# A hybrid mixer layer on one core: the input loaded with channels on the partitions, and three orders stated

## The chip, the core and the metric

The kernel runs on one core of one Trainium2 chip. The metric is device time of one execution in microseconds (us); lower is better. An execution is profiled apart, and its trace is what the views below show. The engines are named as in the profile: PE is TensorE (PEld its weight loads), DVE is VectorE, ACT is ScalarE, POOL is GpSimd, SP is SyncE, which issues most DMAs.

## What is computed

One inference step of one layer with shared weights, over 128 context tokens and 512 latent tokens, 640 together, of width 1024:

```python
def _trunk_layer(x, mod, g_pre, w_in, ...):
    shift, scale, gate = jnp.split(mod, 3, axis=-1)
    h = _rmsnorm(x, g_pre) * (1 + scale) + shift
    proj = h @ w_in
    qa, ka, va, ga, qr, zf, zb, ir, gr, uf, gf = _split_columns(proj)
    ...
    oa = _neighbourhood_attention(...)       # context attention for the context tokens
    o_r, s_fin = _hgrn_bidir(qr, zf, zb, ir, lb_f, lb_b, s0)
    o_r = _rmsnorm(o_r, g_hgrn.reshape(R_HEADS, R_VAL_DIM)).reshape(B, N, R_WIDTH).astype(x.dtype)
    o_f = _fourier(uf, w_fnet)
    mixed = jnp.concatenate([oa * silu(ga), o_r * silu(gr), o_f * silu(gf)], axis=-1)
    out = mixed @ w_out
    return x + gate * _rmsnorm(out, g_post), ka, va, s_fin
```

`mod` is `silu(c) @ w_ada + b_ada`, one vector of 3072 for the context and one for the latent tokens. The first norm is over the 1024 channels of a token: `x * rsqrt(mean(x*x) + 1e-6) * g`.

## The kernel before, in words

All large matrix products are made in single-pass matmuls on operands split into a high and a low part (`hi` and `lo` of a weight, `hT[0]` and `hT[1]` of the modulated input), three matmuls for one product (`mm3`, line 210). An input block of 128 columns is 8 channel tiles x 2 token halves x 3 = 48 matmuls of 128x320.

**The start** (`start_stream`, line 244). The input `x` is loaded with tokens on the partitions, five tiles of 128 tokens, each in two pieces `xa` (640 channels) and `xb` (384 channels) (`load_x`, 217). `scale_x` (222) sums the squares of a tile, `xa` on ScalarE and `xb` on VectorE, takes root and reciprocal, and multiplies the tile by it. Then, for each of the eight channel tiles k, here called a round:

- two blocks of `w_ada` (`wss`, 512 KB each, line 178 loads them) are multiplied with the SiLU of the two conditioning vectors (`mod_cols`, 195, through line 113): 16 matmuls of 32 weight columns, 32 instructions in the trace. This is called the mod group of k;
- VectorE copies the sums (`row`, 266), TensorE transposes the two halves (line 127), VectorE reduces them (272) and makes the scale `G` and the shift (273 to 275);
- `modulated` (233) transposes the five 128x128 pieces of x on TensorE, ScalarE applies scale and shift out of PSUM (237 for the latent tokens, 239 for the context), VectorE makes the high part (240) and the low part (241) of `hT`.

`zf_stream` (286) multiplies each finished channel tile with the first two input blocks, zf0 and zf1, whose weights VectorE and ScalarE split (lines 130, 131): 12 matmuls of 128x320 a round. `fill` (965) then runs the other blocks one after the other, beginning with zb0; `recurrence` (423) and `attention` (645) are streams of their own, put between the blocks' matmuls by modelled times (`Order`, 39), and the framework's scheduler then sets the order on each engine. Engines work their own lists in order.

**The recurrence's states.** After seven levels of 64x128 matmuls, which VectorE merges (458), the chunk states are made: `pst` holds products in one of five PSUM buffers of the tag "b", VectorE copies the final state out (519) and updates the other states one after the other (532), reading `pst`. While it does so the other recurrence's level work (474 to 483) stands in VectorE's list too.

`by_token` (346) copies the last transposed piece of a value tile into a small tile of the pool "m" when `copy_last` is set. Constants (`const`, 137) are loaded by GpSimd's queue, `cc` and `lbl` by SyncE's. The lower bounds `lb` are made first of all (154 to 160).

Of the kernel before, what the change touches and what calls it, by code (L numbers as in the profile page):

```python
# [9 lines left out]
F32 = mybir.dt.float32  # L10
# [3 lines left out]
ALU = mybir.AluOpType  # L14
# [57 lines left out]
def mixer_kernel(ctx: ExitStack, tc: tile.TileContext, A, O):  # L72
# [51 lines left out]

    def tr(out, src):
        od.now += 0.107
        last_tr[0] = te.transpose(out, src, ident).ins  # L127

    def split(src, hi, lo, hi_eng=None, lo_eng=None):
        (sc.copy if hi_eng is None else hi_eng.tensor_copy)(hi, src)  # L130
        (ve if lo_eng is None else lo_eng).tensor_sub(lo, src, hi.bitcast(F32))  # L131
# [15 lines left out]
    sel = const("sel", [2, P])  # L147
# [3 lines left out]


    lb, lb1 = const("lb", [2, 2]), const("lb1", [2, 2])
    ve.tensor_sub(lb, lbl, lbl)
    sc.activation(lb, lb, ACT.Exp)
    ve.reciprocal(lb1, lb)
    ve.tensor_mul(lb, lb, lb1)
    ve.tensor_sub(lb, lb, lb)
    ve.tensor_scalar_max(lb, lb, 0.0)
    ve.tensor_scalar(lb1, lb, -1.0, 1.0, op0=ALU.mult, op1=ALU.add)  # L160
# [10 lines left out]
    sc.activation(csil[:, :, 0:2], cc, ACT.Silu)  # L171

    wdma, nb = [], [1]
# [7 lines left out]
    def split_w(raw, lo_eng=None, shape=(KT, P), tags=("hi", "lo")):  # L181
        hi, lo = [wp.tile([P, *shape], F32R, tag=t, name=nm(t), bufs=WB[t]) for t in tags]
        split(raw, hi, lo, lo_eng=lo_eng)
        return hi, lo
# [10 lines left out]
    def mod_cols(out, w, chain):  # L195

        t = od.now
        for k in range(KT):
            run_mm(chain, out[32 * (k % 4):32 * (k % 4) + 32, :], csil[:, k, :], w[:, k, :], start=(k < 4), stop=(k >= 4))
        od.now = t + 0.45  # L200
# [3 lines left out]
    xa, xb = [T(tag="xa") for _ in range(5)], [T(384, tag="xb") for _ in range(5)]  # L204

    def xcols(i, k):
        return (xa[i] if k < 5 else xb[i])[:, k % 5 * P:k % 5 * P + P]
# [9 lines left out]
    def load_x():  # L217
        for i in range(5):
            load(xa[i], A["x"][i * P:(i + 1) * P, 0:NT])
            load(xb[i], A["x"][i * P:(i + 1) * P, NT:D])  # L220

    def scale_x():
        for i in range(5):
            ss2 = S(2)
            sc.activation(T(), xa[i], ACT.Square, accum_out=ss2[:, 0:1])
            ve.tensor_tensor_reduce(PE_()[:, 0:384], xb[i], xb[i], 1.0, 0.0, op0=ALU.mult, op1=ALU.add,
                                    accum_out=ss2[:, 1:2])
            ve.tensor_add(rstd[:, i:i + 1], ss2[:, 0:1], ss2[:, 1:2])
            rsqrt_mean(rstd[:, i:i + 1], D)
            ve.tensor_scalar(xa[i], xa[i], rstd[:, i:i + 1], 0.0, op0=ALU.mult, op1=ALU.add)  # L230
            ve.tensor_scalar(xb[i], xb[i], rstd[:, i:i + 1], 0.0, op0=ALU.mult, op1=ALU.add)

    def modulated(k, pm):
        h, px = T(), PB()
        for i in range(1, 5):
            tr(px[:, (i - 1) * P:i * P], xcols(i, k))
        sc.activation(h[:, P:NT], px, ACT.Identity, bias=shift[:, k, 1:2], scale=G[:, k, 1:2])
        tr(pm[:, 384:512], xcols(0, k))
        sc.activation(h[:, 0:P], pm[:, 384:512], ACT.Identity, bias=shift[:, k, 0:1], scale=G[:, k, 0:1])
        ve.tensor_copy(hT[0][:, k, :], h)  # L240
        ve.tensor_sub(hT[1][:, k, :], h, hT[0][:, k, :].bitcast(F32))
        od.set(f"h{k}", LAT["h"])

    def start_stream():
        load_x()
# [10 lines left out]
        scale_x()  # L256
        od.now = 11.0
        for k in range(KT):
# [4 lines left out]
            for u in range(2):  # L263
                mod_cols(pm[:, u * P:(u + 1) * P], raws[2 * k + u], [])
            yield 0
            ve.tensor_copy(row, pm[:, 0:256])
            yield LAT["row"]

            for u in range(2):
                tr(pm[:, u * P:(u + 1) * P], row[:, u * P:(u + 1) * P])  # L270
            pt = S(4)
            ve.reduce_sum(pt, pm[:, 0:256].rearrange("p (u g r) -> p u r g", u=2, r=32)[:, :, 0:2, :], axis=AX.X)
            ve.tensor_scalar(G[:, k, :], pt[:, 0:2], bss[:, k, 0:1], 1.0, op0=ALU.add, op1=ALU.add)
            ve.tensor_scalar_mul(G[:, k, :], G[:, k, :], gpre[:, k:k + 1])  # L274
            ve.tensor_scalar_add(shift[:, k, :], pt[:, 2:4], bss[:, k, 1:2])
            modulated(k, pm)
            if k < 2:
                zf_w.append(split_w(zraw[k]))
# [67 lines left out]
    def by_token(src, copy_last=False):  # L346
# [5 lines left out]
        if copy_last:  # L352
            last = S(P)
# [69 lines left out]
    def recurrence(p):  # L423
# [88 lines left out]
        for d in range(2):  # L512
# [5 lines left out]
            for hh in range(2):  # L518
                ve.tensor_copy(fin[RS[hh], :], pst[RS[hh], 64 * hh:64 * hh + 64])
# [3 lines left out]
            for a, i in enumerate(order[d]):  # L523
                for hh in range(2):
# [4 lines left out]
                    else:  # L529
                        ip = order[d][a - 1]  # L530
                        cs = slice((a - 1) * P + 64 * hh, (a - 1) * P + 64 * hh + 64)
                        ve.scalar_tensor_tensor(sall[r, cdst], sall[r, cs], Td[r, ip:ip + 1], pst[r, cdst],  # L532
                                                op0=ALU.mult, op1=ALU.add)
# [319 lines left out]
    def gate_vectors():  # L853
        selr = cp.tile([P, 2, P], F32R, tag="selr", name="selr")
# [219 lines left out]
def prepare(inp):  # L1074
    inp = {k: np.asarray(v) for k, v in inp.items()}
    r = _consts()
    r["x"] = np.concatenate([inp["x_prompt"][0], inp["x_sample"][0]], 0)
    r["cc"] = np.stack([inp["c_ctx"], inp["c"][0]], -1).reshape(KT, P, 2).transpose(1, 0, 2)
# [59 lines left out]
```

## Time and profile before

| | |
|---|---|
| median of 3 runs | 434.32 us (433.76 to 434.38) |
| profiled execution, its own time | 434.13 us |
| its span in the trace | 432.3 us |
| PE busy | 409.4 us (95%) |
| DVE busy | 303.0 us (70%) |
| ACT busy | 205.8 us (48%) |
| HBM read, written | 43.80 MB, 3.28 MB |
| time outside the span (434.13 - 432.3) | 1.8 us |

The trace counts from the span's start. A view of the timeline gives a start, a duration, the engine, the line in the code, what is written and read, and in brackets the idle time ahead of it with what ended it. The chain of waits follows the work that ended last back to the start, so that its pieces leave no gap; for matmuls its pieces are the better measure of a group, since one matmul's own duration overlaps the next one's.

### The profile page before, as it was taken

What the parts mean: (1) busy time and instruction counts of PE and PEld (TensorE: products, weight loads), DVE (VectorE), ACT (ScalarE), POOL (GpSimd) and SP (SyncE); (2) the same over time, 40 slices, a digit from 0 to 9 for tenths busy, and PEclk for the clock granted to TensorE, in tenths of its full rate; (3) what the DMA queues carried; (4) which work ended last, traced back from release to release, by engine and by line L of the source; (5) the groups of instructions that cost most, each with busy time, mean ns of one, the idle gap of its engine ahead of it and who ended that gap; (6) DMA issues with size and microseconds to landing.
All of it is one profiled execution on the core that took longest, in us unless ns stands there. A gap on an engine that the chain in (4) does not pass through costs nothing.

```text
span 432.3 us, 8308 instructions
## 1 busy us (share of the span) xinstructions
PE 409.4 (95%) x3176; PEld 372.6 (86%) x3176; DVE 303.0 (70%) x866; ACT 205.8 (48%) x551; POOL 7.4 (2%) x23
## 2 busy tenths in 40 slices
PE   0699999999998999999999999999999999999994
PEld 0488999999988998999899989899898889988884
DVE  3775579999896966885598657786679748471164
ACT  6525466566342526754445634744466553341331
POOL 2000000000020000000000000000000000000000
PEclk9999999999999999999999999999999999999998
DMA  7996154101202021122012522245323202245032
GB/s 236 414 407 237 49 176 141 61 16 50 99 12 75 9 62 49 56 98 74 33 60 72 143 73 90 90 154 159 105 101 122 89 9 102 85 156 198 0 147 99
DMA packets 19528, 47.62 MB, mean 110 GB/s; under 512 B 3184, under 2 KB 6912, under 8 KB 19488
## 3 DMA queue, kind: packets, MB, share of 16 engines
q1 hardware_dynamic: 19376, 46.94, 31.3%
q8 instruction: 25, 0.41, 0.4%
q0 software_dynamic: 112, 0.14, 0.3%
q14 instruction: 15, 0.12, 0.1%
HBM read 43.80 MB, written 3.28 MB: 109 GB/s over the span
## 4 chain that ended last, share of the span: by engine, by line
PE 90%; DVE 4%; DMA 3%; ACT 1%; issue 0%; SPq 0%; DVEq 0%
PE pb L113 84%; PE pb L127 7%; DMA vs<-wss 1%; DMA txa<-x 1%; DVE t L532 1%; DVE AL L458 1%; DVE AL L495 0%; ACT L688 0%; DVE lo L131 0%; DVE t L960 0%; ACT hi L130 0%; ACT pe L688 0%; ACT pe L689 0%; DVE t L475 0%; DVE t L474 0%
## 5 line engine op out<-in xcount | busy, mean ns | idle before, releaser
L113 PE MATMUL pb<-hT,hi 128*128 128x320 f32 x896 | 207.8, 316 | 0.5 <-DVE t L131 0.4
L113 PEld LDWEIGHTS pb<-hT,hi 128*128 128x128 f32 x896 | 149.5, 188 | 6.4 <-issue 1.1
L113 PE MATMUL pb<-hT,lo 128*128 128x320 f32 x448 | 139.7, 313 | 0.0
L113 PEld LDWEIGHTS pb<-hT,lo 128*128 128x128 f32 x448 | 84.1, 188 | 1.4 <-DVE G L274 0.2
L131 DVE TENSOR_TENSOR lo<-raw,hi 128x1024 fp32r<-128x1024 f32 x35 | 42.7, 1221 | 21.8 <-ACT hi L130 21.5
L130 ACT CAST hi<-raw 128x1024 fp32r<-128x1024 f32 x35 | 36.7, 1049 | 35.2 <-PE pb L113 19.5
L113 PE MATMUL pb<-t,t 64*128 64x128 f32 (+2 forms) x414 | 43.1, 291 | 1.9 <-DVE t L532 1.5
L113 PEld LDWEIGHTS pb<-t,t 64*128 64x128 f32 (+1 forms) x414 | 36.2, 188 | 6.3 <-issue 2.3
L113 PE MATMUL pb<-hi,mh 128*128 128x512 f32 (+1 forms) x108 | 32.1, 376 | 0.0
L130 ACT CAST pT<-pb 128x256 fp32r<-128x256 f32 x64 | 22.9, 371 | 16.3 <-DVE pT L131 9.8
L131 DVE TENSOR_TENSOR pT<-pb,pT 128x256 fp32r<-128x256 f32 x64 | 26.3, 416 | 1.6 <-ACT pT L130 1.3
L113 PEld LDWEIGHTS pb<-hi,mh 128*128 128x128 f32 x108 | 19.4, 189 | 3.2
L113 PE MATMUL pb<-pT,mh 128*128 128x512 f32 (+1 forms) x102 | 22.2, 364 | 0.0
L688 ACT ACTIVATE pe<-pb,s 128x256 f32<-128x256 f32 x32 | 15.2, 476 | 13.0 <-DVE s L687 7.7
L127 PE MATMUL pb<-ident,pe 128*128 128x128 f32 x136 | 20.8, 274 | 0.5 <-ACT pe L689 0.5
L943 ACT ACTIVATE t<-pb 128x512 f32<-128x512 f32 (+1 forms) x11 | 6.0, 551 | 30.5 <-PE pb L113 30.5
L113 PEld LDWEIGHTS pb<-pT,mh 128*128 128x128 f32 x102 | 17.7, 189 | 3.1
L113 PE MATMUL pb<-lo,mh 128*128 128x512 f32 (+1 forms) x54 | 20.2, 373 | 0.0
L127 PEld LDWEIGHTS pb<-ident,pe 128*128 128x128 f32 x136 | 16.5, 140 | 1.7 <-ACT pe L689 0.7
L458 DVE COPY_PREDICATED AL<-masks,pb 128x512 f32<-128x512 uint32 x24 | 16.5, 738 | 1.9 <-PE pb L113 1.8
L113 PE MATMUL pb<-pT,vs 128*128 128x256 f32 (+1 forms) x96 | 17.2, 321 | 0.0
L699 DVE TENSOR_TENSOR o<-pb,o 64x512 f32<-64x512 f32 (+1 forms) x16 | 7.8, 487 | 13.3 <-ACT o L698 13.2
(209 smaller groups left out, 630.1 us busy)
## 6 DMA issues: line engine op xcount, KB each, us to landing
raw<-win SPq DMA_DIRECT2D x30, 512.0 KB, 3.3
pT<-wss SPq DMA_DIRECT2D x12, 512.0 KB, 10.2
raw<-wg SPq DMA_DIRECT2D x8, 512.0 KB, 3.4
raw<-wout SPq DMA_DIRECT2D x8, 512.0 KB, 3.3
t<-x SPq DMA_DIRECT2D x10, 256.0 KB, 5.8
o_y<-t SPq DMA_DIRECT2D x9, 256.0 KB, 2.1
vs<-wss SPq DMA_DIRECT2D x4, 512.0 KB, 9.1
tbl<-tbl SPq DMA_DIRECT2D x4, 512.0 KB, 3.3
```

The lines of the kernel that those rows point to most:

```text
L113: return te.matmul(out, lhsT, rhs, start=start, stop=stop).ins
L127: last_tr[0] = te.transpose(out, src, ident).ins
L130: (sc.copy if hi_eng is None else hi_eng.tensor_copy)(hi, src)
L131: (ve if lo_eng is None else lo_eng).tensor_sub(lo, src, hi.bitcast(F32))
L458: ve.copy_predicated(out, mk.to_broadcast([P, i1 - i0, P]), src)
L532: ve.scalar_tensor_tensor(sall[r, cdst], sall[r, cs], Td[r, ip:ip + 1], pst[r, cdst], op0=ALU.mult, op1=ALU.add)
L688: sc.activation(pe[:, 256:512], ss[:, 256:512], ACT.Exp, bias=m[:, 1:2], accum_out=m[:, 3:4])
L699: ve.tensor_add(out, src[r, :], out)
L943: sc.activation(T(512)[:, cs], po[:, 0:cs.stop - cs.start], ACT.Square, accum_out=ssb[:, j:j + 1])
```

## The change

The input is also prepared as `xT`, eight tiles with 128 channels on the partitions and the 640 tokens along the free axis, and loaded as such, first on SyncE's queue. The 40 transposes of x are gone. The squares of all eight tiles are made on ScalarE, added on VectorE, and summed over the partitions by five small matmuls with a column of ones; root and reciprocal are taken once for all five token tiles; five transposes of a broadcast bring the inverse norms to every partition, and ScalarE copies them to `rb`. VectorE multiplies each `xT` tile by `rb`, one round ahead. ScalarE applies scale and shift from SBUF and, from k = 2 on, also makes the high part of `hT`. `G` is made in one instruction where there were two. The order of these steps on ScalarE, VectorE and TensorE is stated by dependencies without a semaphore (`turn`). `lbl` and `cc` are loaded by ScalarE's queue, `sel` later by SyncE's; the lower bounds are made behind the squares. The states' copies and updates get a high priority on VectorE, and `by_token` copies its last piece in place.

```diff
-    cc = const("cc", [KT, 2], dma=sy.dma_start)
-    lbl = const("lbl", [2, 2], dma=sy.dma_start)
+    xT, x_last = [], None
+    for k in range(KT):
+        xT.append(T(tag="xT"))
+        with tc.issue_after(x_last) if x_last else ExitStack():
+            x_last = sy.dma_start(xT[k], A["xT"][k]).ins
+    lbl = const("lbl", [2, 2], dma=sc.dma_start)
+    cc = const("cc", [KT, 2], dma=sc.dma_start)
...
+    def inverse_norms():
+        acc = T()
+        last = sc.activation(S(1), eps, ACT.Silu)
+        last = turn(sc.activation(acc, xT[0], ACT.Square), last)
+        for k in range(1, KT):
+            sq = T()
+            last = turn(sc.activation(sq, xT[k], ACT.Square), last)
+            added = ve.tensor_add(acc, acc, sq)
+            if k == 4:
+                last = turn(sc.activation(csil[:, :, 0:2], cc, ACT.Silu), last)
+        lower_bounds(last, added)
+        pn = PB()
         for i in range(5):
+            mm(pn[:, 2 * i:2 * i + 2], acc[:, i * P:(i + 1) * P], ones)
+        sc.activation(rstd, pn[...], ACT.Sqrt, bias=eps, scale=1.0 / D)
+        ve.reciprocal(rstd, rstd)
+        return pn
+
+    def spread_norms(pn, prev):
+        pr = PB()
         for i in range(5):
+            tr((pr if i < 4 else pn)[:, i % 4 * P:i % 4 * P + P], rstd[:, i:i + 1].to_broadcast([P, P]))
+            if i == 0:
+                turn_names(last_tr[0], prev)
+        rb = T()
+        sc.copy(rb[:, 0:512], pr)
+        return rb, sc.copy(rb[:, 512:NT], pn[:, 0:P])
...
-        for i in range(1, 5):
-            tr(px[:, (i - 1) * P:i * P], xcols(i, k))
-        sc.activation(h[:, P:NT], px, ACT.Identity, bias=shift[:, k, 1:2], scale=G[:, k, 1:2])
-        tr(pm[:, 384:512], xcols(0, k))
-        sc.activation(h[:, 0:P], pm[:, 384:512], ACT.Identity, bias=shift[:, k, 0:1], scale=G[:, k, 0:1])
-        ve.tensor_copy(hT[0][:, k, :], h)
-        ve.tensor_sub(hT[1][:, k, :], h, hT[0][:, k, :].bitcast(F32))
+        sc.activation(h[:, P:NT], xT[k][:, P:NT], ACT.Identity, bias=shift[:, k, 1:2], scale=G[:, k, 1:2])
+        h_act[0] = sc.activation(h[:, 0:P], xT[k][:, 0:P], ACT.Identity, ...)
+        if k < 2:
+            h_hi[0] = ve.tensor_copy(hT[0][:, k, :], h)
+        else:
+            sc.copy(hT[0][:, k, :], h)
+        return ve.tensor_sub(hT[1][:, k, :], h, hT[0][:, k, :].bitcast(F32))
...
+            row_done = ve.tensor_scalar(G[:, k, :], pt[:, 0:2], bsc1[:, k:k + 1], gpre[:, k:k + 1], op0=ALU.add, op1=ALU.mult)
+            h_done = modulated(k)
+            if k + 1 < KT:
+                turn(ve.tensor_mul(xT[k + 1], xT[k + 1], rb), row_done)
...
-            last = S(P)
+            last = src[:, 4 * P:5 * P]
...
+            with tc.high_priority():
+                for hh in range(2):
+                    ve.tensor_copy(fin[RS[hh], :], pst[RS[hh], 64 * hh:64 * hh + 64])
...
+                        with tc.high_priority():
+                            ve.scalar_tensor_tensor(sall[r, cdst], sall[r, cs], Td[r, ip:ip + 1], pst[r, cdst],
+                                                    op0=ALU.mult, op1=ALU.add)
```

How the change stands in the engines' lists is shown at three places. The numbers behind names are those of buffers and differ between the kernels.

TensorE's list in round 3, before: `vs` and `pT` are the blocks of `w_ada`, `csil` the conditioning vectors, `txa` the tiles of x, `hT` the modulated input, `hi` the weights of zf0 and zf1.

```order
L113 MATMUL pb_347<-pT_197,csil 32x128 x8
L113 MATMUL pb_347<-pT_199,csil 32x128 x8
L127 MATMUL pb_379<-ident,txa_108 128x128
L127 MATMUL pb_379<-ident,txa_109 128x128
L127 MATMUL pb_379<-ident,txa_110 128x128
L127 MATMUL pb_379<-ident,txa_111 128x128
L127 MATMUL pb_300<-ident,txa_107 128x128
L113 MATMUL pb_117<-hT_105,hi_240 128x320
...
L127 MATMUL pb_347<-ident,row_346 128x128 x2
```

The same place in the changed kernel:

```order
L113 MATMUL pb_322<-pT_178,csil 32x128 x8
L113 MATMUL pb_322<-pT_180,csil 32x128 x8
L113 MATMUL pb_115<-hT_113,hi_227 128x320
L113 MATMUL pb_116<-hT_113,hi_227 128x320
...
L136 MATMUL pb_322<-ident,row_321 128x128 x2
L113 MATMUL pb_369<-vs_231,csil 32x128 x8
```

The five transposes of x between the mod group and the zf matmuls are gone, the two of `row` stay.

ScalarE's list around h5, before: `raw_645` is the weight block zb0, `G` and `shift` belong to the round, L283 is a Sigmoid whose table is loaded ahead of use.

```order
L237 ACTIVATE t_425<-pb_426,shift,G 128x512
L239 ACTIVATE t_425<-pb_394,shift,G 128x128
L237 ACTIVATE t_474<-pb_475,shift,G 128x512
L283 ACT_TABLE_LOAD
L283 ACTIVATE s_485<-G 128x1
L239 ACTIVATE t_474<-pb_443,shift,G 128x128
L130 CAST hi_647<-raw_645 128x1024
L237 ACTIVATE t_519<-pb_520,shift,G 128x512
```

In the changed kernel (`txT_86` is the tile of k = 4, `txT_88` of k = 5, `raw_541` is zb0):

```order
L272 ACTIVATE t_399<-txT_86,shift,G 128x512
L273 ACTIVATE t_399<-txT_86,shift,G 128x128
L277 CAST hT_113<-t_399 128x640
L139 CAST hi_543<-raw_541 128x1024
L272 ACTIVATE t_442<-txT_88,shift,G 128x512
L273 ACTIVATE t_442<-txT_88,shift,G 128x128
L330 ACT_TABLE_LOAD
L330 ACTIVATE s_448<-G 128x1
L277 CAST hT_113<-t_442 128x640
L272 ACTIVATE t_487<-txT_90,shift,G 128x512
```

The split of zb0 now stands ahead of h5, where it stood ahead of h6, and each round has a cast more.

TensorE's list near the states of the first recurrence, before: `t,t` matmuls are the last level of the other recurrence, `hT` matmuls belong to input blocks.

```order
L113 MATMUL pb_1566<-t_1481,t_1482 128x128
L113 MATMUL pb_1772<-hT_106,hi_1664 128x320
...
L113 MATMUL pb_1772<-hT_105,lo_1665 128x320
L113 MATMUL pb_1565<-t_1481,t_1482 128x128
L113 MATMUL pb_1838<-hT_105,hi_1834 128x320
```

In the changed kernel:

```order
L113 MATMUL pb_1510<-t_1425,t_1426 128x128
L113 MATMUL pb_1715<-hT_114,hi_1608 128x320
...
L113 MATMUL pb_1715<-hT_113,lo_1609 128x320
L113 MATMUL pb_1781<-hT_113,hi_1777 128x320
...
L113 MATMUL pb_1781<-hT_113,lo_1778 128x320
L113 MATMUL pb_1509<-t_1425,t_1426 128x128
L113 MATMUL pb_1781<-hT_113,hi_1777 128x320
```

The last level matmul (`pb_1565`, now `pb_1509`) had eight `hT` matmuls ahead of it since the one before, and now has 26. On VectorE the copies and updates of the states keep their places between the other recurrence's level steps; two low parts of `vs` and one merge of 128x512 (line 505) now stand among them, ahead of the last update.

More of the change, by code (lines that the diff above doesn't have):

```diff
@@ L127, in tr, with split @@
         last_tr[0] = te.transpose(out, src, ident).ins
[L129 to L131 removed]
+    def split(src, hi, lo, hi_eng=None, lo_eng=None, prev=None, lo_prev=None):
+        ins = (sc.copy if hi_eng is None else hi_eng.tensor_copy)(hi, src)
+        if prev is not None:
+            turn(ins, prev)
+        ins = (ve if lo_eng is None else lo_eng).tensor_sub(lo, src, hi.bitcast(F32))
+        if lo_prev is not None:
+            turn(ins, lo_prev)
     ident = cp.tile([P, P], F32, tag="ident", name="ident")
@@ L141, in const @@
         return t
-    cc = const("cc", [KT, 2], dma=sy.dma_start)
-    lbl = const("lbl", [2, 2], dma=sy.dma_start)
+    xT, x_last = [], None
[5 more added lines that the diff above has]
+    cc = const("cc", [KT, 2], dma=sc.dma_start)
     bss = const("bss", [KT, 2])
     gpre = const("gpre", [KT])
-    sel = const("sel", [2, P])
+    bsc1 = const("bsc1", [KT])
+    ve.tensor_scalar(bsc1, bss[:, :, 0], 1.0, 0.0, op0=ALU.add, op1=ALU.add)
+    ones = cp.tile([P, 2], F32, tag="ones", name="ones")
+    ve.memset(ones, 1.0)
     RS = [slice(0, 64), slice(64, 128)]
@@ L170, in mixer_kernel @@
     gp.memset(csil, 0.0)
-    sc.activation(csil[:, :, 0:2], cc, ACT.Silu)
-    wdma, nb = [], [1]
+    wdma, nb = [x_last], [1]
     def load_raw(src, tag, shape=(KT, P)):
@@ L193, in load, with mod_cols @@
             sy.dma_start(t, src)
-    def mod_cols(out, w, chain):
+    def mod_cols(out, w, chain, prev=None):
         t = od.now
@@ L199, in mod_cols @@
             run_mm(chain, out[32 * (k % 4):32 * (k % 4) + 32, :], csil[:, k, :], w[:, k, :], start=(k < 4), stop=(k >= 4))
+            if k == 0 and prev is not None:
+                turn_names(chain[0], prev)
         od.now = t + 0.45
@@ new lines, in lower_bounds @@
+    def lower_bounds(prev, added):
+        ve.tensor_sub(lb, lbl, lbl)
+        turn(sc.activation(lb, lb, ACT.Exp), prev)
+        turn(ve.reciprocal(lb1, lb), added)
+        ve.tensor_mul(lb, lb, lb1)
+        ve.tensor_sub(lb, lb, lb)
+        ve.tensor_scalar_max(lb, lb, 0.0)
+        ve.tensor_scalar(lb1, lb, -1.0, 1.0, op0=ALU.mult, op1=ALU.add)
+    def inverse_norms():
[10 more added lines that the diff above has]
+        pn = PB()
+        for i in range(5):
+            mm(pn[:, 2 * i:2 * i + 2], acc[:, i * P:(i + 1) * P], ones)
+        sc.activation(rstd, pn[:, 0:10].rearrange("p (i two) -> p i two", two=2)[:, :, 0], ACT.Sqrt, bias=eps, scale=1.0 / D)
+        ve.reciprocal(rstd, rstd)
+        return pn
@@ L853, in gate_vectors @@
     def gate_vectors():
+        sel = const("sel", [2, P], dma=load)
         selr = cp.tile([P, 2, P], F32R, tag="selr", name="selr")
```

67 lines of the change are left out of this document (28 added, 39 removed).

## The prediction

> **What bounds the kernel now.** I read the page first, for which engine fills the span: busy us, share of the span, instructions.
>
> ```profile
> PE 409.4 (95%) x3176; PEld 372.6 (86%) x3176; DVE 303.0 (70%) x866; ACT 205.8 (48%) x551; POOL 7.4 (2%) x23
> ```
>
> Of the span of 432.3 us TensorE idles for 22.9. The view of waits, for TensorE alone, says where.
>
> ```profile
> PE pb L113 <- DMA vs<-wss: 14.0, 1, 14.0
> PE pb L113 <- DVE t L532: 1.5, 1, 1.5
> PE pb L127 <- ACT pe L689: 0.5, 1, 0.5
> ```
>
> 14.0 us lie ahead of its first matmul, which waits for the first block of w_ada, and 1.5 us in the recurrence, where a matmul waits for the state updates of line 532; the attention part loses 0.5. From the first matmul on TensorE is hardly ever without work. So a matmul taken out is worth its own time, if nothing else comes late in its place. Whether it does is a question for the start, so I looked at two stretches of it.
>
> ```profile
> 30.00:35.00 5.00, 5.00 (x81) 4.46 (x83) 2.81 (x10) 1.23 (x2) 0.00 (x0) 1.00 1.03 410
> 40.00:45.00 5.00, 4.99 (x59) 4.27 (x59) 2.85 (x8) 4.57 (x7) 0.00 (x0) 1.00 0.01 3
> ```
>
> The columns are stretch, length, busy time of PE, PEld, DVE, ACT, POOL, granted clock, DMA share, GB/s. In the first the DMAs run full at 410 GB/s, so that a round's 1.05 MB of w_ada takes 2.6 us; in the second they have nothing left to do. TensorE is full in both, and slower than the DMAs: the chain of waits shows a round.
>
> ```profile
> 18.12 1.01 PE pb L113 x16
> 19.14 1.27 PE pb L127 x5
> ...
> 27.03 1.01 PE pb L113 x32
> 28.04 0.70 PE pb L127 x5
> 28.74 1.76 PE pb L113 x12
> ...
> 38.88 0.81 PE pb L127 x6
> ...
> 43.48 0.70 PE pb L113 x4
> ```
>
> Mod group 1.01, twelve zf matmuls 1.76, two row transposes 0.27 (0.81 / 6 is 0.135 each) and five of x 0.68: 3.72 us. The zf matmuls of k = 5 begin at 43.48, 16.45 us after the mod group of k = 3 at 27.03. The first rows go at half pace: sixteen instructions of a mod group took 1.01 us at 18.12, where thirty-two took as much at 27.03, and five transposes 1.27 us at 19.14 and 0.70 at 28.04.
>
> **The change part by part.** *Rounds 3 on.* Of the 40 transposes, by TensorE's list, 25 stand between the mod group of k = 3 and zf of k = 5, and one later: 25 x 0.135 = 3.4 us off TensorE. The other 14 lie in the half-paced start, where something else decides, as follows.
>
> *The front.* These rows of ScalarE carry it.
>
> ```profile
> 3.35 1.28 ACT L171 ACT_TABLE_LOAD   x1
> 4.65 0.22 ACT L171 ACTIVATE csil<-cc 128x16 f32<-128x16 f32 x1
> 5.23 0.74 ACT L225 ACTIVATE t<-txa 128x640 f32<-128x640 f32 x1 [0.36 <-DMA txa<-x]
> ...
> 12.08 0.74 ACT L225 ACTIVATE t<-txa 128x640 f32<-128x640 f32 x1 [0.26 <-DMA txa<-x]
> ```
>
> Before, the first 320 KB of x had landed at 5.23, the fifth such piece at 12.08, with four pieces of 192 KB between: 2.1 MB in 6.9 us, 306 GB/s. The queue's first two DMAs are now on ScalarE's, so x is issued first:
>
> ```profile
> 0.73 0.39 SPq L140 DMA_DIRECT2D cc<-cc  x1
> 1.18 0.42 SPq L140 DMA_DIRECT2D lbl<-lbl  x1
> ```
>
> That is 0.9 us earlier (0.73 in place of 1.6), so the first tile lands at 4.3. Seven more (2.29 MB) take 7.5 us at 306 GB/s or 5.6 at 410: the last lands between 9.9 and 11.8. I take 11.0. One square more, 0.74; then ScalarE loads the Exp table, makes lb, loads the Sqrt table, takes the root. The loads are 1.28 each, the two small activations 0.22 each (4.65): 3.0, to 14.7. Five matmuls with ones lie under that; no row shows one, and I bound them by zero and by the 1.27 of five half-paced transposes. TensorE then makes the first mod group, which waited for its block until 14.0 and now has it about 1 us earlier: twice 1.01 (18.12) from 13.1 is 15.1, with a handover 15.3; five transposes spread the norms, 1.27, to 16.6; ScalarE's two copies, about the 0.78 and 0.45 of the rows below (L237, L239), bring rb to 17.8.
>
> The table load is where a rule speaks against the change: two switches now stand behind the last square. In the rows above the load ends at 4.63 and the next instruction starts at 4.65, so I count 1.28 each. The Trainium skill (ScalarE: Activation LUTs, "What ACT_TABLE_LOAD costs") gives 1283 ns for the load, which agrees, and about 1380 ns of drain besides, which no row here shows; by it the root would be 2.8 us later and the sum about 432.9.
>
> From rb on, VectorE's list decides. Its groups between 26 and 50 us, with busy us and mean ns of one behind the bar:
>
> ```profile
> L241 DVE TENSOR_TENSOR hT<-t,hT 128x640 fp32r<-128x640 f32 x6 | 4.9, 822 | 0.1
> L240 DVE CAST hT<-t 128x640 fp32r<-128x640 f32 x7 | 3.4, 492 | 3.8 <-ACT t L239 3.8
> L266 DVE COPY row<-pb 128x256 f32<-128x256 f32 x6 | 2.5, 420 | 1.0 <-PE pb L113 1.0
> L273 DVE TENSOR_SCALAR G<-s,bss 128x2 f32<-128x2 f32 x6 | 1.4, 227 | 0.1
> ...
> L131 DVE TENSOR_TENSOR lo<-raw,hi 128x1024 fp32r<-128x1024 f32 x1 | 1.2, 1217 | 0.0
> L272 DVE TENSOR_REDUCE s<-pb 128x4 f32<-128x16 f32 x6 | 1.0, 173 | 4.5 <-PE pb L127 4.5
> ```
>
> And ScalarE's in the same stretch:
>
> ```profile
> L237 ACT ACTIVATE t<-pb,shift,G 128x512 f32<-128x512 f32 x7 | 5.4, 778 | 15.5 <-DVE G L274 15.5
> L239 ACT ACTIVATE t<-pb,shift,G 128x128 f32<-128x128 f32 x7 | 3.2, 452 | 2.0 <-PE pb L127 2.0
> L283 ACT ACT_TABLE_LOAD x1 | 1.3, 1283 | 0.0
> L130 ACT CAST hi<-raw 128x1024 fp32r<-128x1024 f32 x1 | 1.0, 1035 | 0.0
> L283 ACT ACTIVATE s<-G 128x1 f32<-128x1 f32 x1 | 0.2, 203 | 0.0
> ```
>
> I price the new multiply of xT by rb as line 241, same shape, 0.82. Until round 2's row is copied VectorE has from 17.8: three multiplies (2.46), three times shift and G (0.45 each, two rounds complete and little left of the first, 0.9), two row copies (0.84), a cast (0.49), a low part (0.82), the weight split (1.22), a reduce (0.17): 6.9, so 24.7. A transposed row later (0.5, handover 0.2) TensorE starts the mod group of k = 3 at 25.5, against 27.03 before. Two zf matmuls are still owed there (0.3).
>
> *With no wait* TensorE would reach zf of k = 5 after 16.45 - 3.4 + 0.3 = 13.4 us, at 38.9, 4.6 earlier than 43.48. There are waits. Round 3's row copy stands behind the cast, reduce, low part, second weight split, shift and G, multiply: 0.49 + 0.17 + 0.82 + 1.22 + 0.45 + 0.82 + 0.42 = 4.4, plus about 0.7 until the reduce has its input: 29.8, where TensorE is through at 25.5 + 1.0 + 2.1 = 28.6. So about 1.2 is lost. Round 4's row follows a reduce, G, multiply, low part and copy, 2.7 with handovers 0.4, from 30.3, about 0.3 more than TensorE's 2.8. Rounds 5 to 7 have enough work ahead. At h5 ScalarE has 0.78 + 0.45, a table load with Sigmoid (1.28 + 0.20) and the cast, bounded by 0.49 (line 240) and 0.74 (line 225), 0.74 taken, in a row: 3.5 from a G at about 37.4, so 41.0. TensorE would be there at 40.5; 0.5 more. I put zf of k = 5 at 41.0: 2.5 gained. One transpose saved later, 0.1, and a similar wait at h7, where little else is ready, 0.5: the start is worth **2.1 us**.
>
> *The recurrence.*
>
> ```profile
> 132.84 0.46 PE L113 MATMUL pb<-t,t 64*128 64x128 f32 x2 [1.53 <-DVE t L532]
> ...
> 133.35 1.39 DVE L458 COPY_PREDICATED AL<-masks,pb 128x512 f32<-128x512 uint32 x2
> ...
> 134.90 0.22 DVE L131 TENSOR_TENSOR vs<-m,vs 128x64 fp32r<-128x64 f32 x1
> ```
>
> The matmul that waits has no data from the states; it needs a PSUM buffer, which they still read. "States first" does not come out in the list: the copies and updates keep their places, and three instructions are new among them, two low parts (as at 134.90) and one merge (one of the two at 133.35): 2 x 0.22 + 0.7 = 1.1 us later for the last update. But 18 more hT matmuls stand ahead of the waiting one, 18 x 0.147 = 2.6 (1.76 / 12), against 1.53 + 1.1 = 2.6: the wait goes, **1.5 us**, and with nothing to spare.
>
> *At nothing:* the split of G into one instruction, lb made later (first used after zf, past 44 us, made by 17), sel behind ten blocks, by_token's copy in place (a small tile less to wait for). In the attention part the order is shuffled at some sixty places; TensorE waits 0.5 us there in all, so it can give at most that, and a stall like the longest of before, 1.5, bounds the other side. I take zero.
>
> Sum: 2.1 + 1.5 = 3.6 us. Against the profiled execution's own 434.13 (span 432.3 and 1.8 around it) that is **430.5 us**; the median of the runs shown, 434.32, stands 0.2 above that execution, less than I can tell apart.
>
> **The rivals.**
>
> *TensorE never waits (0.18).* If steps on VectorE overlap better than their durations, the start gives 4.6, with the recurrence 6.1: 428.0 us. For it: VectorE was busy for only 2.8 of the 5 us from 30 to 35, and its list a round is about as long now. Against it: two weight splits in the two rounds that matter.
>
> *The front is no earlier (0.15).* If x lands as late as before, or the half pace lasts a round longer, zf of k = 5 moves by 1.5: 432.0 us. For it: fewer matmuls early. At 18.12 and 19.14 TensorE was still at half pace, 5 us after its first matmul. The Trainium skill (TensorE: Matmul & The Clock Gate, "What's actually happening") has full pace after about 3.4 us of sustained work, by which a late front could not come from the clock. This trace doesn't bear the 3.4 out.
>
> *The tables cost the drain too (0.03).* If ScalarE is held after each of the two loads by as much again, the root comes 2.6 later; 0.4 of that lies under the mod group, which ends at 15.3, so everything behind moves by 2.2: 432.7 us. The gap of 0.02 above speaks against it.
>
> *The recurrence's wait stays, and the new order of the attention part stalls once (0.08).* Each 1.5: 433.5 us, no change.
>
> *ScalarE blocked by zb0 (0.06): slower.* The cast of zb0 now stands ahead of h5, and ScalarE's list is worked in order. If the block lands at L, h5's high part is there at L + 1.04 + 0.78 + 0.45 + 1.28 + 0.20 + 0.74 = L + 4.5.
>
> The whole gain is gone when that reaches 44.6, L = 40.1; the kernel is slower by more than 0.2% from L = 41 on, and at L = 42 the time is 430.5 + 46.5 - 41.0 = 436.0. Against it: before, all that was queued had landed by 40 (DMA share 0.01 in the stretch after), zb0 behind the masks, which now come behind it. I expect L near 36.
>
> **How the numbers follow.** My forecast has 0.50, 430.5 us. A run tells about 0.2% from no change, 0.9 us, so faster means under 433.4: forecast, no waits, late front and tables, 0.50 + 0.18 + 0.15 + 0.03 = 0.86; same 0.08; slower 0.06. The range reaches down to the case without waits and most of the attention part's 0.5, 427.6, and up to the case where wait and stall stay, 433.6; the blocked ScalarE lies outside.
>
> **What would show it.** Right: no L127 transposes from tiles of x; mod group of k = 3 near 25.5, zf of k = 5 near 41; TensorE idle 2 us in all between 28 and 50, put down to VectorE's row copies and ScalarE's cast; no wait over 0.3 near line 581. Wrong: TensorE idle over 4 us before 50, ended by the cast of zb0; a mod group of 1.0 per 16 after 27 us; a busy sum of TensorE that falls by less than 4.

## The result, and the profile after

The changed kernel takes 429.58 us (median of 4 executions, 429.09 to 430.5), the kernel before 434.04 beside it (433.7 to 434.38): a ratio of 0.990, 95% interval 0.988 to 0.9919. The profiled execution took 429.5 with a span of 427.7, so that 1.8 lie outside the span, as before. The executions of the kernel before lie in two heaps by granted clock, 433.2 us in the middle at 0.996 and more (called the early heap below), 434.6 at 0.994 and less (the late heap); that moves its median from one set of runs to the next (433.5 to 434.1), and differences under 0.5 us between kernels of different sets mean nothing here.

The first line of the page:

```profile
PE 405.9 (95%) x3151; PEld 370.5 (87%) x3151; DVE 305.6 (71%) x840; ACT 212.2 (50%) x554; POOL 7.3 (2%) x22
```

TensorE's busy time fell by 3.5 us, the span by 4.6 (432.3 to 427.7). The other 1.1 is idle time. The view of waits for TensorE (line, what it waited for, sum, times, longest):

```profile
PE pb L113 <- DVE t L246: 12.4, 1, 12.4
PE pb L136 <- DVE row L306: 1.6, 2, 0.9
PE pb L113 <- DVE hT L279: 0.4, 1, 0.4
PE pb L113 <- DVE AL L505: 0.3, 1, 0.3
```

TensorE starts at 12.4 in place of 14.0. The 1.5 us behind the state updates are gone, and so is the attention part's 0.5; new are 1.6 behind two row copies (VectorE's copy of the mod group's sums, `row`) and 0.4 behind a low part. The same stretches of the start as before, and the one where the row copies are waited for:

```profile
20.00:25.00 5.00, 3.50 (x44) 2.49 (x44) 4.73 (x10) 2.57 (x5) 0.40 (x1) 1.00 1.03 406
...
30.00:35.00 5.00, 4.61 (x81) 3.78 (x70) 4.34 (x12) 2.88 (x5) 0.00 (x0) 1.00 1.02 406
40.00:45.00 5.00, 4.89 (x58) 4.63 (x59) 3.12 (x7) 2.98 (x6) 0.00 (x0) 1.00 0.36 108
```

Before, TensorE was full in all three (4.94 and 5.00 and 4.99) and VectorE half empty (2.79 and 2.81 and 2.85). Now VectorE is full from 20 to 25 (4.73 of 5) and TensorE waits 1.5 us of it. Rows of the timeline, in time order:

```profile
12.40 2.30 PE L113 MATMUL pb<-ones,t 128*128 128x2 f32 x10 [12.40 <-DVE t L246]
14.74 0.27 ACT L253 ACTIVATE rstd<-pb,eps 128x5 f32<-128x5 f32 x1 [0.90 <-PE pb L113]
16.50 1.33 PE L136 MATMUL pb<-ident,rstd 128*128 128x128 f32 x5
18.43 0.82 DVE L310 TENSOR_TENSOR txT<-txT,t 128x640 f32<-128x640 f32 x1
20.70 0.44 PE L136 MATMUL pb<-ident,row 128*128 128x128 f32 x2 [0.85 <-DVE row L306]
25.21 0.44 PE L136 MATMUL pb<-ident,row 128*128 128x128 f32 x2 [0.75 <-DVE row L306]
25.58 1.08 PE L113 MATMUL pb<-pT,csil 128*32 128x128 f32 x32
29.35 0.44 PE L136 MATMUL pb<-ident,row 128*128 128x128 f32 x2
36.20 1.04 ACT L139 CAST hi<-raw 128x1024 fp32r<-128x1024 f32 x1
41.11 1.15 PE L113 MATMUL pb<-hT,hi 128*128 128x320 f32 x6
118.97 0.17 DVE L538 TENSOR_SCALAR s<-pb 128x10 f32<-128x10 f32 x1
131.87 0.49 PE L113 MATMUL pb<-t,t 64*128 64x128 f32 x2
421.17 0.28 PE L113 MATMUL pb<-lo,mh 128*128 128x256 f32 x1
```

The mod group of k = 3 starts at 25.58 and zf of k = 5 at 41.11, where 25.5 and 41.0 were forecast. The matmul that had waited 1.53 us for the state updates stands at 131.87 without a wait. The row at 118.97 (line 538, line 491 before) serves as a marker below: it is the last step of the recurrence's levels, far behind the start and ahead of everything that the later order touches, since behind the start the engines' lists first differ at 124 us. With the last matmul it cuts each execution into a start and a rest.

### The profile page after: what moved, and what is told of

Same layout as the page of the kernel before. It is cut to its first block, busy times and chain, and to the rows that moved or that the text cites. A ratio compares the mean times of both kernels' runs of the same rounds, so it can differ in the third digit from the quotient of the medians.

```text
span 427.7 us, 8220 instructions
## 1 busy us (share of the span) xinstructions
PE 405.9 (95%) x3151; PEld 370.5 (87%) x3151; DVE 305.6 (71%) x840; ACT 212.2 (50%) x554; POOL 7.3 (2%) x22
## 4 chain that ended last, share of the span: by engine, by line
PE 89%; DVE 5%; ACT 3%; DMA 1%; issue 1%; SPq 0%; DVEq 0%; ACTq 0%
PE pb L113 84%; PE pb L136 5%; DMA txT<-xT 1%; ACT t L272 1%; DVE t L246 1%; DVE hT L279 1%; DVE lo L142 1%; ACT hT L277 0%; DVE AL L505 0%; ACT t L273 0%; SPq L161 0%; DVE shift L318 0%; DVE AL L542 0%; ACT L330 0%; DVE G L319 0%
## 5 line engine op out<-in xcount | busy, mean ns | idle before, releaser
L139 ACT CAST pT<-pb 128x256 fp32r<-128x256 f32 x64 | 23.2, 371 | 30.1 <-DVE pT L142 18.9
L113 PE MATMUL pb<-hi,mh 128*128 128x512 f32 (+1 forms) x108 | 30.6, 375 | 0.0
L113 PE MATMUL pb<-lo,mh 128*128 128x512 f32 (+1 forms) x54 | 19.3, 375 | 0.0
L748 DVE TENSOR_TENSOR o<-pb,o 64x512 f32<-64x512 f32 (+1 forms) x16 | 7.8, 488 | 12.6 <-ACT o L747 12.5
```

The source lines that it names most:

```text
L113: return te.matmul(out, lhsT, rhs, start=start, stop=stop).ins
L139: ins = (sc.copy if hi_eng is None else hi_eng.tensor_copy)(hi, src)
L748: ve.tensor_add(out, src[r, :], out)
```

## The experiments

### Which edit moved the recurrence and the attention part

Three kernels take the change apart. The first is the changed kernel with the old copy in `by_token`:

```diff
-            last = src[:, 4 * P:5 * P]
+            last = S(P)
```

> The changed kernel, but by_token copies its last piece into a small tile again. My theory: this copy in place is what moved the last level matmul behind 26 hT matmuls, so that taking it back brings the wait of about 1.5 us on the state updates (line 580 or so) back, and the attention part's 0.5 to 0.9: 429.6 + 1.5 + 0.9 = 432.0 us, with the recurrence's diagonal row still near 119.0 (the start keeps its 2.0). Rival, as my prediction had priced the copy: nothing, 429.6 us.

The second is the kernel before with the copy in place and the two `high_priority` blocks, and nothing else:

```diff
-            last = S(P)
+            last = src[:, 4 * P:5 * P]
...
+            with tc.high_priority():
...
+                        with tc.high_priority():
```

> The kernel before with two pieces of the change alone: the copy in place and the high priority of the states. My theory: 434.0 - 1.5 - 0.9 = 431.6 us, no wait behind the state updates, the start unchanged (mod group of k = 3 near 27.0). Rival (the gain of the change comes from the start alone): 434.0 us.

The third is the changed kernel without the two blocks:

```diff
-            with tc.high_priority():
...
-                        with tc.high_priority():
```

> The changed kernel without the high priority of the states' copies and updates. My theory: the priority changes no order on any engine, so the same time, 429.6 us. Rival (states first is what takes the wait away): 1.5 us more, 431.1 us.

Measured, all in one set with the kernel before at 434.09: with the old copy 432.75 us (432.16 to 434.39, 12 executions; ratio to before 0.9977, interval 0.9963 to 0.9992); the kernel before with the copy in place and priority 430.38 (430.17 to 430.89; 0.9917, 0.9898 to 0.9936); without priority 429.9 (429.59 to 430.43; 0.9905, 0.9888 to 0.9923). The first is 0.75 above my 432.0, the second 1.2 below my 431.6, the third at its 429.6 within the noise; none of the three rivals held. Side by side, in medians:

| | old copy | copy in place |
|---|---|---|
| old input and start | 434.09 | 430.38 |
| new input and start | 432.75 | 429.9 |

So the new input, which names the change, gives 1.3 us with the old copy and 0.5 with the copy in place; the copy gives 3.7 and 2.9.

TensorE's waits with the old copy, where three from the old order are back (lines 581, 738 and 142; 532, 689 and 131 before):

```profile
PE pb L113 <- DVE t L581: 1.5, 1, 1.5
...
PE pb L136 <- ACT pe L738: 0.5, 1, 0.5
PE pb L113 <- DVE t L142: 0.4, 1, 0.4
```

All of TensorE's waits in the kernel before with copy in place and priority:

```profile
PE pb L113 <- DMA vs<-wss: 13.9, 1, 13.9
PE pb L113 <- DVE AL L458: 0.4, 1, 0.4
```

And the marker with the last matmul, first of the kernel before:

```profile
120.97 0.17 DVE L491 TENSOR_SCALAR s<-pb 128x10 f32<-128x10 f32 x1
...
426.07 0.28 PE L113 MATMUL pb<-lo,mh 128*128 128x256 f32 x1
```

of the changed kernel with the old copy:

```profile
118.92 0.17 DVE L538 TENSOR_SCALAR s<-pb 128x10 f32<-128x10 f32 x1
...
423.83 0.28 PE L113 MATMUL pb<-lo,mh 128*128 128x256 f32 x1
```

and of the kernel before with copy in place and priority:

```profile
120.22 0.17 DVE L491 TENSOR_SCALAR s<-pb 128x10 f32<-128x10 f32 x1
...
422.33 0.28 PE L113 MATMUL pb<-lo,mh 128*128 128x256 f32 x1
```

From marker to last matmul it is 305.10 us before and 304.91 with the old copy, but 302.11 and, in the changed kernel (118.97 to 421.17), 302.20 with the copy in place. Without priority it is 302.21. So the copy in place is worth 2.7 to 3.0 us of these stretches whatever the start looks like, and the priority nothing: the lists of the engines are the same with it and without. From 60 us on the lists of TensorE, VectorE and ScalarE (numbers of buffers left out) are the same in the kernel before and the changed kernel with the old copy, and the same in the two kernels with the copy in place, so nothing else of the change reaches that far. Of the 2.7, the three waits make 2.4 (1.5 + 0.5 + 0.4); the other 0.3 stands in no wait that the trace shows.

ScalarE's row of the copy shows what the small tile did, first in the kernel before, then in the changed kernel:

```profile
132.79 0.27 ACT L354 COPY m<-pb 128x128 f32<-128x128 f32 x1 [6.03 <-DVE t L532]
...
123.95 0.26 ACT L401 COPY t<-pb 128x128 f32<-128x128 f32 x1
```

Before, the copy waited 6.03 us for the state updates of line 532, which read tiles of the same pool "m"; in the changed kernel with the old copy it waits 6.04 for line 581 again. In place it waits for nothing and comes some 7 us ahead of the place it had, and with it the split of the value tile. How the scheduler gets from there to the other order on TensorE, with 18 hT matmuls more ahead of the last level matmul and some sixty places changed behind it, was not followed. In the list of the kernel with the old copy there are eight again.

The difference between the starts is smaller than the two first profiles say: 120.97 before against 118.97 is 2.0, but the kernel before with the copy in place, whose start is that of before, has its marker at 120.22. That called for more profiles of the kernel before.

### The kernel before, twice more

Both runs are of the unchanged kernel, so there is no edit.

> The kernel before, unchanged, for a second profile. Its 17 runs beside the first experiments lie in two heaps: 8 with a mean granted clock of 0.996 or 0.997 (432.6 to 434.1 us) and 9 with 0.992 to 0.994 (434.0 to 434.8). My theory: in the second heap the 1.5 us in which TensorE waits for the state updates halves its clock for about 3.4 us, which costs 1.7 us (0.004 of 432 us); an execution at 434.4 or more shows a granted clock near 0.5 in a stretch right behind line 532's wait, one near 432.7 shows none. Rival: the late heap comes from the start, where half pace lasts longer; then the diagonal row of line 491 stands at 122 or later in a late execution and the clock is 1.00 behind the wait.

> The kernel before, unchanged, for a third profile, since the second fell into the early heap (433.28 us, clock 0.996, 1.00 behind line 532's wait). My theory as there: an execution of the late heap (434.4 or more, clock 0.994 or less) shows the clock near 0.5 for about 3.4 us behind the 1.5 us wait. Rival: it shows a late start and full clock. An execution of the early heap would leave it open.

Both fell into the early heap: 433.28 us with clock 0.996, and 433.1 with 0.997. Neither shows a clock under 1.00 behind line 532's wait, so what makes the late heap is left open: no profile of it was had. The 56 executions of the kernel before that ran beside the experiments are 37 at 0.996 to 0.998 (median 433.2) and 19 at 0.992 to 0.994 (median 434.6). The six of the kernel before with the copy in place are all at 0.996 or more. One time at half clock as shown below, 1.7 us lost, is 0.004 of the time, which is the difference of the two clocks; that is an argument and no proof. The four executions profiled with that wait show none.

What the profiles do show is that the start varies, with the same lists on all engines. Two rows of the third profile:

```profile
18.32 1.02 PE L113 MATMUL pb<-pT,csil 128*32 128x128 f32 x16
19.27 0.77 PE L127 MATMUL pb<-ident,txa 128*128 128x128 f32 x5
```

Here five transposes take 0.77 at 19.27, full pace; in the first profile a group of 16 was still at half pace at 22.57 (1.02, against 0.64 in the second profile at 22.39). The mod group of k = 3 began at 26.96 (27.03 by the chain of waits), 26.40 and 26.17 in the three profiles and at 26.21 in the kernel before with the copy in place; the marker stood at 120.97, 120.41, 120.17 and 120.22. The prediction had taken its base from the latest of the four. With the new input the marker stands at 118.97, 118.92 and, without priority, 119.77. The means are 120.4 and 119.2: the start is worth 1.2 us, with a scatter of 0.8 on each side. Of that 0.3 is given back behind the last matmul, where all kernels with the new input take 6.2 to 6.3 us to the end of the span, and those with the old one 6.0; why is open. The 0.9 that is left lies between the 1.3 and 0.5 of the medians above.

### Transposes put back

```diff
             row_tr = last_tr[0]
+            if k >= 3:
+                for i in range(5):
+                    tr(pm[:, 384:512], xT[k][:, i * P:(i + 1) * P])
```

> The changed kernel with the five transposes a round put back on TensorE from k = 3 on: they transpose the tile xT[k] into an unused part of a PSUM buffer, and nobody reads the result. 25 transposes, 25 x 0.135 = 3.4 us of TensorE's time. My theory: TensorE idles about 2.5 us between 25 and 50 us, behind VectorE's and ScalarE's lists, so most of the transposes fill idle time and about 1.3 us is added: 430.9 us, zf of k = 5 at 42.3. Rival one (TensorE sets the pace there, as in the kernel before): the full 3.4, 433.0 us. Rival two (another engine sets the pace alone): 429.6 us.

Measured: 432.19 us (431.84 to 432.3; ratio 0.9956, 0.9939 to 0.9974), 2.3 to 2.6 more than without them. That lies between my 1.3 and the full 3.4. The zf matmuls of k = 5 begin at 43.27, not at 42.3. The marker, here with that of the kernel without priority below it, stands at 121.68:

```profile
121.68 0.17 DVE L541 TENSOR_SCALAR s<-pb 128x10 f32<-128x10 f32 x1
...
119.77 0.17 DVE L538 TENSOR_SCALAR s<-pb 128x10 f32<-128x10 f32 x1
```

It is 2.7 behind the changed kernel's and 1.9 behind that of the kernel without priority, which is the fairer one, since both ran part of the start at half clock. A stretch of each, first with the transposes:

```profile
21.00:26.00 5.00, 4.74 (x46) 3.60 (x45) 4.68 (x9) 2.10 (x3) 0.40 (x1) 0.66 1.04 406
```

and without priority:

```profile
21.00:26.00 5.00, 4.61 (x43) 3.45 (x44) 4.46 (x10) 2.39 (x4) 0.40 (x1) 0.66 1.04 408
```

A mean of 0.66 over 5 us is 3.4 us at 0.50: 0.34 x 5 = 1.7 us of full-speed work lost. Such a time at 0.50 is called a spell below. It came behind a wait for a row copy of 1.57 us in the one and 1.32 in the other; the changed kernel waited 0.85 there and kept 1.00 (above, 20 to 25). So the transposes gave 1.9 to 2.7 of their 3.4 us. And a marker at 121.68 against 120.2 to 120.4 of the old start (one was at 120.97) says that the new front without these saved transposes would be slower than the old one, by about 1.3. The medians say the same, 432.19 against 430.38 for the old start with the same order behind it: 1.8, of which 0.3 lies at the end of the span. The spell may be part of it, since the old start had none. What the new front has to pay for, I think, are squares, norms, their spreading, and VectorE's longer list; the shares were not taken apart.

### What the front hangs on

The lower bounds first, as before:

```diff
+    lb, lb1 = const("lb", [2, 2]), const("lb1", [2, 2])
+    ve.tensor_sub(lb, lbl, lbl)
+    sc.activation(lb, lb, ACT.Exp)
...
-        lower_bounds(last, added)
```

> The changed kernel, but the lower bounds are made first of all, as before, so that only one table is loaded behind the squares. My theory: nothing, 429.6 us: the spreading transposes stand behind the mod group, which ends at 16.5, and the reciprocal was there at 15.2, so that the 1.3 us saved lie under TensorE's work. Rival (the two tables set the front): 1.3 to 1.5 less, 428.2 us, rb at 17.1.

Measured: 431.04 us (430.64 to 431.72; ratio 0.9944, 0.9928 to 0.996), 1.4 slower than the changed kernel, which neither theory had. ScalarE's timeline shows why:

```profile
3.17 1.28 ACT L176 ACT_TABLE_LOAD   x1
4.46 0.20 ACT L176 ACTIVATE lb<-lb 128x4 f32<-128x4 f32 x1
...
9.06 1.28 ACT L245 ACT_TABLE_LOAD   x1
10.35 0.22 ACT L245 ACTIVATE csil<-cc 128x16 f32<-128x16 f32 x1
10.47 1.97 ACT L242 ACTIVATE t<-txT 128x640 f32<-128x640 f32 x3
```

The SiLU in the midst of the squares now needs its table again, since Exp has put it out; the last three squares and the ones behind them come 1.57 later (13.97 in place of 12.40), and the mod group of k = 3 1.35 later (26.93). So the second table load behind the squares was not what held the front up: in the changed kernel both are through at 13.84, and the root waits until 14.74 for the matmuls with ones (its 0.90 above). A load among the squares does hold it up, and this later front (the marker 1.36 later, at 120.33) was later at the end in full.

The multiply of xT by rb on GpSimd:

```diff
-                turn(ve.tensor_mul(xT[k + 1], xT[k + 1], rb), row_done)
+                gp.tensor_mul(xT[k + 1], xT[k + 1], rb)
```

> The changed kernel with the multiply of xT by rb on GpSimd in place of VectorE (five of 128x640 a little ahead of need, 0.83 us each on VectorE). My theory: VectorE's list makes the two waits behind the row copies (0.9 and 0.8 us), so they shrink by about 0.8 each and TensorE keeps its clock: 428.4 us, mod group of k = 3 near 24.3. Rival one: GpSimd takes 2 us or more for one, and h comes later: 431 us. Rival two: the waits come from TensorE's own pace, no change, 429.6.

Measured: 438.39 us (437.15 to 438.89; ratio 1.0114, 1.0095 to 1.0133), far above all three forecasts. VectorE's groups from 18 to 32 us (busy us, mean ns of one behind the bar):

```profile
L319 DVE TENSOR_SCALAR G<-s,bsc,gpre 128x2 f32<-128x2 f32 x2 | 3.1, 1574 | 0.0
L318 DVE TENSOR_SCALAR shift<-s,bss 128x2 f32<-128x2 f32 x2 | 2.8, 1401 | 0.0
L142 DVE TENSOR_TENSOR lo<-raw,hi 128x1024 fp32r<-128x1024 f32 x1 | 2.6, 2562 | 0.0
L279 DVE TENSOR_TENSOR hT<-t,hT 128x640 fp32r<-128x640 f32 x1 | 2.1, 2061 | 0.0
```

In the changed kernel the same groups have 281, 279, 1218 and 823 ns. GpSimd takes 1.85 us for a multiply (seven in 12.96, from 18.41 to 31.37), and while it works some of VectorE's instructions take two to nearly six times as long. TensorE waits 3.3 and 2.7 us for two row copies:

```profile
22.00:28.00 6.00, 4.72 (x41) 3.51 (x42) 5.02 (x5) 2.14 (x3) 6.00 (x5) 0.50 1.06 394
```

and its clock is at 0.50 for these six us as well. The multiplies did leave VectorE's list, but in this stretch the four groups above took 7.4 us more for it than at their old prices, and the four multiplies that the changed kernel makes there are worth 3.3. So the test doesn't say what a shorter list on VectorE would be worth.

The norms spread by the matmul itself:

```diff
-    ones = cp.tile([P, 2], F32, tag="ones", name="ones")
+    ones = cp.tile([P, P], F32, tag="ones", name="ones")
...
+        mm(pr, ones, acc[:, 0:512])
+        mm(pn[:, 0:P], ones, acc[:, 512:NT])
+        sc.activation(rb[:, 0:512], pr, ACT.Sqrt, bias=eps, scale=1.0 / D)
+        last = sc.activation(rb[:, 512:NT], pn[:, 0:P], ACT.Sqrt, bias=eps, scale=1.0 / D)
+        ve.reciprocal(rb, rb)
```

> The changed kernel with the norms summed and spread in one step: the 128x128 ones are the stationary operand, so that every partition gets the sums of the squares; root on ScalarE and reciprocal on VectorE are then of 128x640, and the five transposes and ScalarE's two copies go. My theory: rb comes about 1 us earlier (17.4 in place of 18.4) if the reciprocal of 640 columns takes about 0.8 us, and the time falls by 1.0 to 428.6 us. Rival: the reciprocal takes over 2 us, rb is later and the time 430.5.

Measured: 433.43 us (432.36 to 434.68; ratio 0.9993, 0.9978 to 1.0009). The rival held in kind, though the time is 2.9 above its 430.5:

```profile
15.47 4.15 DVE L255 RECIPROCAL t<-t 128x640 f32<-128x640 f32 x1 [1.94 <-ACT t L254]
```

The root is there at 15.4, but the reciprocal takes 4.15 us, five times a multiply of that shape, and TensorE waits 3.30 for the row copy behind it, with its clock halved for the 6.8 us after that wait.

### Filling TensorE ahead of the ones

```diff
         pn = PB()
+        for i in range(32):
+            te.transpose(pn[:, 384:512], ident, ident)
```

> The changed kernel with 32 transposes of the identity on TensorE ahead of the five matmuls with ones, from about 3.3 us on, while it has nothing to do; nobody reads the result, and the mod group of k = 0 is kept behind the ones. My theory: the start runs at half pace because TensorE comes out of idleness, so that the filling brings the ones to about 1.2 us in place of 2.30, the first mod groups and the spreading transposes to half; rb comes near 16.4 in place of 18.40, and since a front 1.57 later had cost 1.4, 2.0 earlier gives 1.8 less: 427.8 us. Rival one: the pace doesn't depend on what ran before, the ones take 2.3 again: 429.6. Rival two: the first block of w_ada or VectorE's list takes up what is won: 429.0 to 429.6.

The same with ScalarE's row copies:

```diff
-            row_copy = ve.tensor_copy(row, pm[:, 0:256])
-            if k:
-                turn(row_copy, row_done)
+            row_copy = sc.copy(row, pm[:, 0:256]) if k else ve.tensor_copy(row, pm[:, 0:256])
```

> As the kernel with the 32 transposes, and from k = 1 on the copies of row are made by ScalarE in place of VectorE (0.42 us each off VectorE's list in the rounds where TensorE waits for them). My theory: VectorE's list makes these waits, so TensorE gains up to 0.8 more on that kernel: 427.0 us. Rival: in ScalarE's list the copies stand behind h and the casts, and h of the next round behind them, so that one wait takes the other's place: no better than it, 427.8 or more.

And that with a longer filling:

```diff
-        for i in range(32):
+        for i in range(58):
```

> As the kernel with row copies on ScalarE, with 58 transposes of the identity in place of 32: those had ended at 8.7, TensorE then stood idle for 4.1 us, and the granted clock was 0.50 from 14 to 17.5. 26 more at 0.135 reach 12.2, where the ones begin between 12.4 and 13.1. In ScalarE's list the copy of round 1's row now stands ahead of h0. My theory: without that idleness the clock stays at 1.00, the ones take about 1.2, the mod groups 0.55 each and the spreading 0.66; rb comes near 16.2 in place of 18.0, and of these 1.8 us some 1.5 reach the end: 428.4 us. Rival: what follows is bound by the chain over rb, h0 and its cast, the idleness moves behind the first mod groups, and the clock is halved there instead, for 3.4 us: 429.6 to 430 us, no gain.

Measured: 430.82 us (430.29 to 431.6; ratio 0.994, 0.9922 to 0.9959), 429.98 (428.93 to 430.47; 0.9912, 0.9894 to 0.9931) and 429.29 (428.64 to 430.29; 0.9906, 0.9887 to 0.9926). None can be told from the changed kernel as better; the first is slower, above its theory and both rivals. The three forecasts of a gain (427.8, 427.0, 428.4) all missed. With 32 transposes:

```profile
3.00:9.00 6.00, 5.68 (x32) 5.44 (x32) 2.48 (x5) 3.55 (x6) 0.15 (x1) 1.00 1.01 347
9.00:13.00 4.00, 0.00 (x0) 0.00 (x0) 3.58 (x5) 3.83 (x6) 0.00 (x0) 1.00 1.03 415
14.00:17.00 3.00, 3.00 (x40) 2.48 (x40) 0.85 (x4) 0.83 (x2) 0.00 (x0) 0.52 1.02 410
```

32 transposes in 5.68 us are more than 32 x 0.135 = 4.3 and less than twice that, so the pace rose during the filling, and the ones took 1.40 in place of 2.30. But 4.2 us of idleness lie between the two, and from 14.1 on the clock was at 0.5, so that the mod group of k = 0 was no faster than without the filling (1.08 for 16). Besides, the ones began at 13.10 with 32 transposes and at 13.31 with 58, in place of 12.40, because ScalarE waited longer for tiles of x; why these landed later is not shown. With 58 transposes, which end at 12.6:

```profile
12.00:15.00 3.00, 2.27 (x35) 2.02 (x37) 2.00 (x7) 2.96 (x4) 0.00 (x0) 1.00 1.03 418
16.00:19.00 3.00, 2.87 (x37) 1.91 (x35) 2.02 (x6) 1.75 (x4) 0.00 (x0) 0.50 1.03 408
20.00:22.00 2.00, 0.27 (x2) 0.28 (x3) 1.93 (x6) 2.00 (x5) 0.00 (x0) 1.00 1.01 402
23.00:26.00 3.00, 3.00 (x34) 2.60 (x24) 2.97 (x4) 0.37 (x1) 1.00 (x1) 0.50 1.03 408
```

The ones took 1.28, the two halves of the first mod group 0.64 and 0.62, and the first multiply by rb came at 17.59, 0.84 earlier. Yet the clock was halved at 16 all the same, with only 0.73 us of idleness ahead of the ones, and again behind 1.9 us of waiting for the first cast of h at 19.8 to 21.7. That is the rival's account: the chain over rb, h0 and its cast sets the pace there, and a TensorE that is through earlier waits longer. That it loses its clock because of these waits fits the order in time and is not shown. That ScalarE's row copies help (0.8 less than with VectorE's, in one set of runs) speaks for VectorE's list as what makes the waits; the two kernels' lists differ in more than that, so it is not shown.

## Why the prediction came out as it did

430.5 us was forecast, 429.58 measured. The parts stand otherwise than forecast.

*TensorE bounds the kernel; a matmul taken out is worth its time if nothing else comes late.* It held with its condition: other things came late in their place. Of 25 transposes, 3.4 us, 1.9 to 2.7 came out, and the new front cost part of that again.

*The front.* The times on the new side were right (25.58 for 25.5, 41.11 for 41.0), though by other steps: the last square ended at 11.03 where 11.7 was reckoned, the ones took 2.30 where 1.27 was the bound and held up root and mod group, rb was 0.6 later than 17.8, and the waits behind row copies came in rounds 1 and 2 (0.85, 0.75) and not in round 3, where 1.2 had been put and row stands at 29.35 without a wait. The step that failed here is the base: 27.03 for the mod group of k = 3 and 43.48 for zf of k = 5 came from one execution, in which half pace had lasted longest. The term of 2.1 us is 1.2, less 0.3 at the end of the span.

*Two tables behind the squares at 1.28 each, without the drain.* Right: the loads at 11.04 and 12.56 took 1.28 each, and lb's Exp followed the first at 12.34. The edit that made lb later was put at nothing; made first it costs 1.4 us, because the SiLU table would be loaded twice.

*The wait in the recurrence goes, 1.5 us, since 18 hT matmuls more stand ahead of the waiting one; "states first" does nothing to the list.* Both held, and the copies and updates of the states stay where they were. But the 18 matmuls come from the copy in place, as the next point has it.

*By_token's copy in place at nothing, the attention part at zero.* This is the step that was wrong. The copy in place is the only cause of the new order behind the start, so the 1.5 us belong to it, and with them 1.2 us more: 0.5 and 0.4 of waits in the attention part and behind a low part, and 0.3 that stays open. The prediction saw the one place and the sixty others in the lists and put them down to the change as a whole, without asking which edit made them; and it took the small tile for a tile to wait for, but put no price on that wait, which was 6.03 us on ScalarE.

*ScalarE blocked by zb0.* The cast stands at 36.20, right behind the one of h4, with no wait for its block: the block was there by the 36 that I expected.

*What would show it.* A busy sum falling by less than 4 was to count as wrong, and it fell by 3.5. By this sign the account of the start was wrong: the ones (2.30, with 1.27 as their bound) and the spreading (1.33) cost more at half pace than I had counted on. Between 28 and 50 TensorE idled 0.7 us, not 2, but 1.5 between 20 and 25.

The sum: 1.2 + 2.7 - 0.3 = 3.6 us between executions at the same clock, which takes the early heap of before, 433.2, to 429.6. The forecast of 3.6 had the same size by luck: the start was 1.2 too good in it, and the order 1.2 too small. The forecast's 430.5 stands 0.9 above 429.58 because it was taken from 434.13, that one execution, and not from 433.2. The 4.5 between the medians has 0.9 more than the sum, which goes with the late heap of the kernel before; of the profiled executions without the recurrence's wait, those at a clock under 0.995 all had it halved in the start.

## What to carry to other kernels

Where a scheduler sets the order, compare the lists edit by edit: an edit that looks like housekeeping (a tile less) may move more than the one that is named for it, and a priority may move nothing. Cross the edits, each with and without the others, before a gain is put down to the one that gives the change its name. Take the base of a forecast from several profiles, above all for the first microseconds, where one execution here was 0.8 us later than another. When a bounded engine gets less to do in a stretch, look at who feeds it there, and whether its clock drops after the new idleness.

## What the runs showed of the hardware

- TensorE's granted clock has two values in these traces, 1.00 and 0.50, and a spell at 0.50 lasts 3.4 us (without priority, with transposes, with all three fillings) or 6.8 (norms by matmul, and the first of two with the multiply on GpSimd). The Trainium skill (TensorE: Matmul & The Clock Gate, "What's actually happening") has a free-running window of 3413 ns, and one or two of those agree with these lengths. In these traces no length of idleness decides: 1.32 and 1.57 us were followed by a spell, 1.64 (32 transposes, at 18.9), 0.97 (lower bounds first) and the recurrence's 1.53 were not, and a spell came 2.5 us behind 0.73.
- The half pace from the first instruction on (a group of 16 in 1.08, until 19 to 24 us) is not in the granted clock, which shows 1.00 there.
- Beside multiplies of 128x640 on GpSimd some VectorE instructions are longer, the tiny ones more than five times (281 to 1574 ns). A row copy out of PSUM (0.41 at 22.00) and a reduce (0.16 at 28.42) among them kept their time; so did a multiply (824 ns), but it had begun 0.05 us ahead of GpSimd's first.
- A reciprocal of 640 columns takes 4.15 us, a multiply of the same shape 0.82.
- The matmuls with two columns of ones take as long as transposes of 128 columns: ten instructions take 2.30 us at half pace and 1.28 at full, 0.13 each, where a transpose takes 0.135.
